# Low halves of weight blocks on GpSimd instead of VectorE, four blocks fewer left unsplit, and one more head searched early

## The chip, the core and the metric

The kernel runs on one core of one Trainium2 chip. The core has five engines that run side by side, each through its own queue in order: TensorE (PE, with its weight loads shown as PEld), VectorE (DVE), ScalarE (ACT), GpSimd (POOL) and SyncE (SP, which only issues DMAs). An engine waits for another by semaphores. The metric is the device time of one execution in microseconds; lower is better.

## The reference

One layer of an encoder block for 512 tokens of width 1024, float32. First a mixer (gated convolution and a gated recurrence in parallel), which ends in a residual add. Then the part that matters here, a retrieval of experts:

```python
q = (xb @ w_q).reshape(p, 8, 2, 64)                      # 8 heads, two half queries
sc = jnp.einsum('phcd,hcnd->phcn', q, sub_keys)           # 128 scores per half
top_s, top_i = lax.top_k(sc, 16)                          # the 16 best of each half
cand_s = top_s[:, :, 0, :, None] + top_s[:, :, 1, None, :]
best_s, best_pos = lax.top_k(cand_s, 16)                  # the 16 best of 256 sums
g = jax.nn.softmax(best_s, axis=-1)
act = gelu(einsum('phkd,pd->phk', expert_u[idx], xb))     # idx: one of 16384 experts
out = einsum('phk,phkd->pd', g * act, expert_v[idx])
```

After it come a residual add and a final normalization.

## The kernel before

*Split products.* The kernel multiplies on PE in a float32 form (FR) that keeps only part of the mantissa. To stay exact it splits a weight block `raw` (128 x 1024) into a high half, the value rounded to FR by an ACT copy (`high`, L75), and a low half, `raw - high`, one subtraction on DVE (`low`, L80). `mm3` then multiplies high by high, high by low and low by high (L89, L90, L91). A block may also stay unsplit: its matmuls in plain float32 (L1039) take longer on PE, but no high or low is needed.

*Phases.* After the mixer, the query phase (L594 to L618): for each of the 8 heads PE projects the queries (`ps_z`), ACT copies them, PE forms the scores (L612), ACT copies those to `sc` (L618; eight buffers, two of them a head). DVE starts on the searches: for one head and one tile of 128 tokens, `top16` finds the 16 best of both halves (MAX8, FIND_INDEX8, MATCH_REPLACE8; L570 to L579; it yields after each of two halves of the work). `early` does this for the first HQ heads and all four tiles. Here a scheduler orders the instructions.

Then the expert phase. The first 64 + 128 tokens (192) are handled sparsely, by gathering expert rows; the other 320 densely: all 128 blocks of `expert_u` are multiplied by the 320 tokens (`u_chunk`), one block of 128 experts each, 123 of them here (block 0 runs in the query phase). Blocks 1 to FN - 1 stay unsplit. Beside them DVE does what is left of the searches (`stage1` for heads HQ to 7, tile 1 first), the selection of each tile (`topk_tile`: candidates L664, best of the candidates, one-hot chains L704 to L709 for the two index halves `ij`, the weights `g`), the gates (one-hot matrices `oh` L755, `igh` L769, multiplied on PE to `ps_gt`, L788, copied by ACT and stored), and the dots of the sparse tokens (L946). POOL gathers expert rows by indirect DMA (`gath`, L925) into five buffers. When `idx_b` (the indices of the first sparse tokens, L715) is planned, the loop emits four gathers. Two loop passes later PE transposes `ij` and `g` (`ps_t`, L730, L731).

Then the vector phase: `expert_v` blocks are weighted into `acc` (L1225), while DVE finishes dots and sums the gathered rows (`ys`, L963).

*What sets the order.* In the expert phase the order is written by a planner in program order: for each block `k` it issues loads, the low of block `k + 2`, the matmuls of `k`, the high of `k + 3`, and then fills DVE from four generators (searches `s`, rest `r`, gates `g`, dots `d`) until DVE's planned time has caught up with PE's. It uses fixed costs:

```python
pe[0] += FPE if c and k < FN else 3530
dve[0] += 0 if c and k < FN - 2 else 1140
while dve[0] < RHO * pe[0] or k == KD:
```

*Buffers.* Raw blocks live in `wraw` (four slots), highs in `whi`, lows in `wlo` (four each). A slot of `wraw` is free for the next load when high and low of its block are formed. Unsplit blocks from number 5 on are loaded into `whi` and `wlo` slots instead.

Of the kernel before, what the change touches and what calls it, by code (L numbers as in the profile page):

```python
# [8 lines left out]
F32 = mybir.dt.float32  # L9
# [25 lines left out]
def block_kernel(ctx, tc, xT, small, w_ada1, w_ada, b_ada, w_in, w_r, w_i, w_out, w_q, keys, uT, u, v, final_g, out):  # L35
    nc = tc.nc
# [31 lines left out]
    def load_w(src):  # L68
        raw = wring.tile([128, KB, 128], F32, name="wraw", bufs=WR)
        nc.sync.dma_start(raw, src)  # L70
        return raw

    def high(raw):
        hi = wring.tile([128, KB, 128], FR, name="whi", bufs=WB)
        nc.scalar.activation(hi, raw, AF.Copy)  # L75
        return hi

    def low(raw, hi):
        lo = wring.tile([128, KB, 128], FR, name="wlo", bufs=WB)
        nc.vector.tensor_sub(lo, raw, hi.bitcast(F32))  # L80
        return lo

    def split_w(raw):
        hi = high(raw)
        return hi, low(raw, hi)

    def mm3(ps, hi, lo, xh, xl, ks, first, last):
        for k in ks:
            nc.tensor.matmul(ps, hi[:, k, :], xh(k), start=first and k == ks[0], stop=False)  # L89
            nc.tensor.matmul(ps, hi[:, k, :], xl(k), start=False, stop=False)  # L90
            nc.tensor.matmul(ps, lo[:, k, :], xh(k), start=False, stop=last and k == ks[-1])  # L91
# [299 lines left out]
    for cb in range(4):  # L391
# [35 lines left out]
        h = mt("ig")  # L427
# [50 lines left out]
    qraw, qsp = {}, {}  # L478
    for m in range(KB):
# [13 lines left out]
        hi, lo = osp.pop(m)  # L493
# [90 lines left out]
    def stage1(heads, tiles):  # L584
        for t in tiles:
            for h in heads:
                yield from top16([(top[:, t, h, c], ti[:, t, h, c], sc[h, c][:, t, :]) for c in range(2)], 128, 1000)

    early = chain(*(stage1([h], range(NT)) for h in range(HQ)))

# [3 lines left out]
    for h in range(8):  # L594
        if h + 2 < 8:
            qraw[h + 2] = load_w(w_q[h + 2])
        else:
            qraw[h + 2] = load_w(uT[h - 6])
        if h:
            qsp[h + 1] = split_w(qraw[h + 1])  # L600
        hi, lo = qsp[h]
        ps = psZ.tile([128, T], F32, name="ps_z", bufs=3)
        mm3(ps, hi, lo, lambda k: h2h[:, k, :], lambda k: h2l[:, k, :], range(KB), True, True)
        if h == 7:
            ps0 = psZ.tile([128, NU], F32, name="ps_z", bufs=3)
            mm3(ps0, *qsp[8], hd, ld, range(KB), True, True)
        qT = qp.tile([128, T], F32, name="qT")
        nc.scalar.activation(qT, ps, AF.Copy)
        pss = [psZ.tile([128, NT, 128], F32, name="ps_g", bufs=2) for c in range(2)]
        for t in range(NT):  # L610
            for c in range(2):
                nc.tensor.matmul(pss[c][:, t, :], qT[64 * c:64 * c + 64, t * 128:(t + 1) * 128],  # L612
                                 keys_sb[64 * c:64 * c + 64, h, :], start=True, stop=True)
        for _ in range(6 if h >= 2 else 0):
            next(early, None)
        for c in range(2):
            sc[h, c] = scs.tile([128, NT, 128], F32, name="sc", bufs=SCB)
            nc.scalar.activation(sc[h, c], pss[c], AF.Copy)  # L618
# [147 lines left out]
    def settle():  # L766
        while lazy:
            o, a, b = lazy.pop(0)
            nc.vector.tensor_tensor(o, a, b, op=OP.mult)  # L769
# [74 lines left out]
    def searches_E():  # L844
        heads = range(HQ, 8)
        yield from stage1(heads, [1])
        yield from topk_tile(1)
        while not gopen:
            yield None
        for t in (2, 3, 0):  # L850
            yield from topk_tile(t)
        sready.append(0)

    def rest_E():
        yield from stage1(range(HQ, 8), [2, 0, 3])
        scx.close()
        stgp.append(ep.enter_context(tc.tile_pool(name="stgp", bufs=1, side="right")))
        gopen.append(cur[0])
# [117 lines left out]
    wraw, whi, wlo = {1: qraw[9]}, {}, {}  # L976
# [3 lines left out]
    def w_load(k):  # L980
        if k < len(jobs):
            kind, i = jobs[k]
            if 5 <= k < FN:
                raw = wring.tile([128, KB, 128], FR, name=("wlo", "whi")[k % 2], bufs=WB).bitcast(F32)
# [11 lines left out]
    def w_high(k):  # L996
        if FN <= k < len(jobs):
            whi[k] = high(wraw[k])

    def w_low(k):  # L1000
        if FN <= k < len(jobs):
            wlo[k] = low(wraw.pop(k), whi[k])
            settle()

    loaded = [4]
# [6 lines left out]
    def weights(k):  # L1012
        w_ahead(k)
        w_low(k + 2)
# [4 lines left out]
    def spill(q):  # L1019
        nc.sync.dma_start(Ad[q], act[q].rearrange("p c t -> p (c t)"))  # L1020
        act[q] = None
# [3 lines left out]
    def u_evict():  # L1025
        if unread:
            c, ps = unread.pop()
            if c % 2 == 0:
                act[c // 2] = ring.tile([128, 2, NU], F32, name="act", bufs=RB // 2)
            nc.scalar.activation(act[c // 2][:, c % 2], ps, AF.Gelu)  # L1030

    def u_chunk(k, pool):
        c = jobs[k][1]
        if c:
            ps = pool.tile([128, NU], F32, name="ps_act", bufs=3 if pool is psE else 2)
            if k < FN:
                raw = wraw.pop(k)
                for j in range(KB):
                    nc.tensor.matmul(ps, raw[:, j, :], h2f[j // 2][:, j % 2], start=j == 0, stop=j == KB - 1)  # L1039
            else:  # L1040
                mm3(ps, whi.pop(k), wlo.pop(k), hd, ld, range(KB), True, True)
            u_evict()
            unread.append((c, ps))
        q = c // 2 - 2
        if c % 2 == 0 and 0 <= q < v0 // 2:
            spill(q)
        pe[0] += FPE if c and k < FN else 3530
        dve[0] += 0 if c and k < FN - 2 else 1140
        ac[0] += 450 if c and k < FN - 3 else 1400

    gbuf, g16, gdone = {}, {}, set()
# [69 lines left out]
    pe, dve, ac = [0], [-HEAD], [0]  # L1121
# [27 lines left out]
    for k in range(1, 3):  # L1149
        w_high(k)  # L1150
    w_low(1)
    manual = ExitStack()
    manual.enter_context(tc.manual_schedule())
    for k in range(CE):
        weights(k)
        u_chunk(k, psE)
        if k >= CE - 2:
            (v_gated, v_high)[k - CE + 2](0)
# [82 lines left out]
    for k in range(CE, len(jobs)):  # L1241
# [5 lines left out]
        if kind == "v" and n % 2:  # L1247
            v_rest(n // 2 + 1)
        w_low(k + 2)
        if kind == "u":  # L1250
            u_chunk(k, psP)
# [71 lines left out]
GS = 32768.0  # L1323
AB = 3
GPE = 460
FN = 12
DX = 0.3
FPE = 4400
SE = 0.65
# [18 lines left out]
WB = 4  # L1348
WR = 4
SCB = 8  # L1350
HQ = 4
VT = 4


# [45 lines left out]
```

## Time and profile before

| | us |
|---|---|
| median of 3 runs | 1334.07 (1334.02 to 1335.56) |
| the profiled execution | 1335.26 |
| its span | 1333.5 |
| PE busy | 1297.6 |
| DVE busy | 1219.9 |
| ACT busy | 728.8 |
| POOL busy | 501.9 |

In the span, the query projections end and the first unsplit block begins at 283.14, and the vector phase begins at 785.9. A line of a time line has start, length, engine, source line, operation, output and inputs, and in brackets the idle time before it with what ended it. A group line has the summed busy time and the mean length in ns. An `x16` behind a matmul counts records: an unsplit block of 8 matmuls has 16.

### The profile page before, as it was taken

The numbers are of one execution on the slowest core, as the hardware profiler recorded it, in microseconds if no ns is written. First come the engines' busy times: TensorE is split into PE (matmuls) and PEld (weight loads), VectorE is DVE, ScalarE is ACT, GpSimd is POOL, SyncE is SP. The second block draws the span as 40 slices with busy tenths as digits, with TensorE's granted clock in tenths as the row PEclk, the third lists the DMA queues.
The fourth block names the chain that finished last, engine by engine and source line by source line (L and its number), as shares of the span: only waits on it lengthen the run. The fifth ranks groups of instructions, "written<-read, shape, count | busy, mean of one in ns | idle before, by whom it ended". The sixth has DMA issues, their size and how long they took to land.

```text
span 1333.5 us, 21104 instructions
## 1 busy us (share of the span) xinstructions
PE 1297.6 (97%) x7408; PEld 1116.0 (84%) x7408; DVE 1219.9 (91%) x2258; ACT 728.8 (55%) x1319; POOL 501.9 (38%) x336
## 2 busy tenths in 40 slices
PE   5999999999899999999999999999999999999996
PEld 2678777777899999999999998888888888888885
DVE  6899876899999999999889769899989989899998
ACT  4667735424686987978659643333343434333333
POOL 0000001000144123456555627677656555555540
PEclk9999999999999999999999999999999999999998
DMA  9684552252799899999999999999999999999993
GB/s 364 228 302 157 165 152 90 69 190 87 254 361 349 316 340 357 390 402 403 418 394 416 418 349 397 390 398 416 412 415 413 415 412 416 412 414 411 412 360 136
DMA packets 150266, 440.03 MB, mean 330 GB/s; under 512 B 16016, under 2 KB 43664, under 8 KB 150160
## 3 DMA queue, kind: packets, MB, share of 16 engines
q1 hardware_dynamic: 103008, 267.23, 53.7%
q0 software_dynamic: 46864, 170.41, 32.4%
q8 instruction: 58, 0.95, 0.3%
q10 hardware_dynamic: 288, 1.05, 0.2%
q14 instruction: 48, 0.39, 0.1%
HBM read 393.54 MB, written 45.09 MB: 329 GB/s over the span
## 4 chain that ended last, share of the span: by engine, by line
PE 74%; DVE 17%; issue 3%; DMA 2%; ACT 2%; POOL 0%; SPq 0%; DVEq 0%; ACTq 0%; POOLq 0%
PE acc L1225 38%; PE ps_act L89 6%; PE ps_act L90 6%; PE ps_act L91 6%; PE ps_z L90 4%; PE ps_z L89 4%; PE ps_z L91 4%; DVE wlo L80 4%; DVE oh L755 2%; DVE scr L946 2%; PE ps_gt L788 2%; DMA wraw<-in_uT_dram 1%; DVE rep L574 1%; DVE igh L769 1%; ACT igh L776 1%
## 5 line engine op out<-in xcount | busy, mean ns | idle before, releaser
L75 ACT ACTIVATE whi<-wraw 128x1024 fp32r<-128x1024 f32 x255 | 269.6, 1058 | 226.7 <-DMA wraw<-in_v_dram 101.4
L80 DVE TENSOR_TENSOR wlo<-wraw,whi 128x1024 fp32r<-128x1024 f32 x255 | 311.1, 1220 | 42.7 <-ACT whi L75 41.7
L89 PE MATMUL ps_act<-h,whi 128*128 128x320 f32 x928 | 292.1, 315 | 0.0
L91 PE MATMUL ps_act<-h,wlo 128*128 128x320 f32 x928 | 287.5, 310 | 0.9 <-DVE wlo L80 0.9
L90 PE MATMUL ps_act<-h,whi 128*128 128x320 f32 x928 | 287.3, 310 | 0.0
L925 POOL DMA_INDIRECT rows<-in_u_dram,idx_s x128 | 206.4, 1612 | 141.7 <-DVE scr L946 112.0
L925 POOL DMA_INDIRECT rows<-in_v_dram,idx_s x128 | 196.6, 1536 | 156.8 <-DVE ys L963 136.1
L1225 PE MATMUL acc<-whi,cl 128*128 128x512 f32 x744 | 229.1, 389 | 0.0
L1225 PE MATMUL acc<-whi,ch 128*128 128x512 f32 x744 | 229.1, 389 | 0.0
L1225 PE MATMUL acc<-wlo,ch 128*128 128x512 f32 x744 | 229.0, 389 | 0.0
L91 PEld LDWEIGHTS ps_act<-h,wlo 128*128 128x128 f32 x928 | 174.6, 188 | 1.3 <-DVE wlo L80 1.1
L89 PEld LDWEIGHTS ps_act<-h,whi 128*128 128x128 f32 x928 | 174.8, 188 | 0.6
L90 PEld LDWEIGHTS ps_act<-h,whi 128*128 128x128 f32 x928 | 174.9, 188 | 0.2
L925 POOL DMA_INDIRECT rows<-in_u_dram,idx_b x64 | 92.5, 1446 | 218.2 <-DVE scr L946 154.9
L963 DVE SCALAR_TENSOR_TENSOR ys<-rows,acts,ys 128x1024 f32<-128x1024 f32 x127 | 163.4, 1287 | 1.4
L1225 PEld LDWEIGHTS acc<-whi,cl 128*128 128x128 f32 x744 | 139.6, 188 | 29.1
L1225 PEld LDWEIGHTS acc<-wlo,ch 128*128 128x128 f32 x744 | 139.6, 188 | 29.0
L1225 PEld LDWEIGHTS acc<-whi,ch 128*128 128x128 f32 x744 | 139.4, 188 | 28.7
L946 DVE SCALAR_TENSOR_TENSOR scr<-rows,h2n 128x1024 f16<-128x1024 f32 x128 | 156.5, 1222 | 4.8 <-DMA rows<-in_u_dram,idx_s 3.2
L1030 ACT ACTIVATE act<-ps_act 128x320 f32<-128x320 f32 x127 | 55.5, 437 | 106.2 <-PE ps_act L91 73.2
L1109 ACT ACTIVATE ch<-cf 128x768 fp32r<-128x768 f32 x64 | 54.2, 847 | 90.9 <-issue 51.8
L776 ACT ACTIVATE igh<-oh,gl 128x128 f16<-128x128 f16 x320 | 99.5, 430 | 7.7 <-DVE oh L755 7.6
(320 smaller groups left out, 1862.6 us busy)
## 6 DMA issues: line engine op xcount, KB each, us to landing
wraw<-in_uT_dram SPq DMA_DIRECT2D x120, 512.0 KB, 7.4
wraw<-in_v_dram SPq DMA_DIRECT2D x103, 512.0 KB, 13.5
Gd<-stg SPq DMA_DIRECT2D x46, 512.0 KB, 9.4
wada<-in_w_ada_dram SPq DMA_DIRECT2D x45, 512.0 KB, 5.3
Ad<-act SPq DMA_DIRECT2D x48, 320.0 KB, 7.7
act<-Ad SPq DMA_DIRECT2D x48, 320.0 KB, 14.4
raw<-in_v_dram SPq DMA_DIRECT2D x25, 512.0 KB, 13.2
h<-Gd SPq DMA_DIRECT2D x12, 1024.0 KB, 17.7
```

The lines of the kernel that those rows point to most:

```text
L75: nc.scalar.activation(hi, raw, AF.Copy)
L80: nc.vector.tensor_sub(lo, raw, hi.bitcast(F32))
L89: nc.tensor.matmul(ps, hi[:, k, :], xh(k), start=first and k == ks[0], stop=False)
L90: nc.tensor.matmul(ps, hi[:, k, :], xl(k), start=False, stop=False)
L91: nc.tensor.matmul(ps, lo[:, k, :], xh(k), start=False, stop=last and k == ks[-1])
L776: nc.scalar.activation(ig[:, 1, k // 2, :, k % 2], of[:, k // 2, 0, :, k % 2], AF.Copy, scale=gl[:, t0 + k:t0 + k + 1])
L925: nc.gpsimd.indirect_dma_start(out=r[:, :], out_offset=None, in_=table, in_offset=bass.IndirectOffsetOnAxis(ap=idxs[:, k:k + 1], axis=0))
L946: nc.vector.scalar_tensor_tensor(scr, rows.pop(n), 1.0, hn, op0=OP.mult, op1=OP.mult, accum_out=dst[:, k:k + 1])
L963: nc.vector.scalar_tensor_tensor(ys, rows.pop(k), acts[:, k:k + 1], ys, op0=OP.mult, op1=OP.add)
L1030: nc.scalar.activation(act[c // 2][:, c % 2], ps, AF.Gelu)
L1109: nc.scalar.activation(ch, coef[q], AF.Copy)
L1225: nc.tensor.matmul(accs[b][e], st[:, bs], mv[:, e * 512:(e + 1) * 512], start=first, stop=last)
```

## The change

The query weights of heads 2 to 7 and block 0 of `expert_u` get their lows on POOL (seven subtractions), and so do blocks 8 to 17 (`k < PL`). FN falls from 12 to 8, so that blocks 8 to 11 are split like the later ones. HQ rises from 4 to 5: the fifth head's four searches move into the query phase, which takes seven search steps a head instead of six. The planner counts no DVE time for the lows on POOL.

```diff
-    def low(raw, hi):
+    def low(raw, hi, eng=None):
         lo = wring.tile([128, KB, 128], FR, name="wlo", bufs=WB)
-        nc.vector.tensor_sub(lo, raw, hi.bitcast(F32))
+        (eng or nc.vector).tensor_sub(lo, raw, hi.bitcast(F32))
...
-            qsp[h + 1] = split_w(qraw[h + 1])
+            qsp[h + 1] = split_w(qraw[h + 1], nc.gpsimd)
...
-        for _ in range(6 if h >= 2 else 0):
+        for _ in range(7 if h >= 2 else 0):
...
-            wlo[k] = low(wraw.pop(k), whi[k])
+            wlo[k] = low(wraw.pop(k), whi[k], nc.gpsimd if k < PL else None)
...
-        dve[0] += 0 if c and k < FN - 2 else 1140
+        dve[0] += 0 if c and k < max(FN, PL) - 2 else 1140
...
-FN = 12
+FN = 8
+PL = 18
...
-HQ = 4
+HQ = 5
```

POOL's queue from the end of the mixer on. `x1d` is the residual stored for the end, `ssum` a zero for one first gather, `idx_b` and `idx_s` the indices of the two sparse groups. Before:

```order
L475 DMA x1d<-xn 128x512 x8
L646 MEMSET ssum 128x8
L647 DMA rows<-in_u_dram,ssum 128x1024
L925 DMA rows<-in_u_dram,idx_b 128x1024 x64
L925 DMA rows<-in_u_dram,idx_s 128x1024 x69
```

Now:

```order
L475 DMA x1d<-xn 128x512 x8
L80 TENSOR_TENSOR wlo<-wraw,whi 128x1024 x7
L646 MEMSET ssum 128x8
L647 DMA rows<-in_u_dram,ssum 128x1024
L80 TENSOR_TENSOR wlo<-wraw,whi 128x1024 x6
L925 DMA rows<-in_u_dram,idx_b 128x1024 x4
L80 TENSOR_TENSOR wlo<-wraw,whi 128x1024 x4
L925 DMA rows<-in_u_dram,idx_b 128x1024 x60
```

The seven lows of the query phase, then those of blocks 8 to 13, stand ahead of the first four gathers; those of blocks 14 to 17 stand between these and the other sixty.

DVE at the end of tile 1's selection, the second one-hot chain (`oh`, `ij`) and the indices. Before:

```order
L579 MAX_INDEX ti<-top,rep 128x8 x2
L80 TENSOR_TENSOR wlo<-wraw,whi 128x1024
L704 TENSOR_TENSOR oh<-oh,io_2644 128x2048
L705 TENSOR_TENSOR oh<-oh,tif 128x2048
L708 TENSOR_TENSOR oh<-oh 128x128x8
L708 TENSOR_TENSOR oh<-oh 128x128x4
L708 TENSOR_TENSOR oh<-oh 128x128x2
L709 TENSOR_TENSOR ij<-oh 128x128
L80 TENSOR_TENSOR wlo<-wraw,whi 128x1024
L712 SCALAR_TENSOR_TENSOR best<-ij 128x128
L715 CAST idx_b<-best 64x64 x2
```

Now:

```order
L574 MATCH_REPLACE rep<-top,sc 128x128 x2
L704 TENSOR_TENSOR oh<-oh,io_2692 128x2048
L705 TENSOR_TENSOR oh<-oh,tif 128x2048
L708 TENSOR_TENSOR oh<-oh 128x128x8
L708 TENSOR_TENSOR oh<-oh 128x128x4
L708 TENSOR_TENSOR oh<-oh 128x128x2
L709 TENSOR_TENSOR ij<-oh 128x128
L712 SCALAR_TENSOR_TENSOR best<-ij 128x128
L715 CAST idx_b<-best 64x64 x2
```

Two lows (of blocks 12 and 13) are gone from this place, and the second half of a search (L577, L579) that stood ahead of the chain now stands behind it.

PE at the transposes of `ij` and `g`; `ps_act_3144` is block 13, `ps_act_3197` block 14. Before:

```order
L91 MATMUL ps_act_3144<-h2_83,wlo_3053 128x320
L730 MATMUL ps_t_3173<-ident_73,ij_2839 128x128 x2
L731 MATMUL ps_t_3173<-ident_73,g_2829 128x128
L89 MATMUL ps_act_3197<-h2_83,whi_3066 128x320
L90 MATMUL ps_act_3197<-h2_83,whi_3066 128x320
L91 MATMUL ps_act_3197<-h2_83,wlo_3089 128x320
```

Now, with `ps_act_3207` block 12 and `ps_act_3244` block 13:

```order
L91 MATMUL ps_act_3207<-h2_83,wlo_3116 128x320
L730 MATMUL ps_t_3236<-ident_73,ij_2862 128x128 x2
L731 MATMUL ps_t_3236<-ident_73,g_2852 128x128
L89 MATMUL ps_act_3244<-h2_83,whi_3145 128x320
L90 MATMUL ps_act_3244<-h2_83,whi_3145 128x320
L91 MATMUL ps_act_3244<-h2_83,wlo_3164 128x320
```

The transposes moved up by one block. The first two gate sets (L788) follow block 17 and block 18 before, and block 16 and block 17 now.

More of the change, by code (lines that the diff above doesn't have):

```diff
@@ L76, in high, with split_w @@
         return hi
-    def low(raw, hi):
+    def low(raw, hi, eng=None):
         lo = wring.tile([128, KB, 128], FR, name="wlo", bufs=WB)
-        nc.vector.tensor_sub(lo, raw, hi.bitcast(F32))
+        (eng or nc.vector).tensor_sub(lo, raw, hi.bitcast(F32))
         return lo
-    def split_w(raw):
+    def split_w(raw, eng=None):
         hi = high(raw)
-        return hi, low(raw, hi)
+        return hi, low(raw, hi, eng)
     def mm3(ps, hi, lo, xh, xl, ks, first, last):
```

## The prediction

> **What bounds the kernel now.** I read first the page's head and busy times, then the work of each stretch, then TensorE's (PE's) waits in the expert phase, then the time lines of PE, VectorE (DVE), ScalarE (ACT) and GpSimd (POOL) where the change sits.
>
> ```profile
> span 1333.5 us, 21104 instructions
> PE 1297.6 (97%) x7408; PEld 1116.0 (84%) x7408; DVE 1219.9 (91%) x2258; ACT 728.8 (55%) x1319; POOL 501.9 (38%) x336
> ```
> ```profile
> 283.14:361.89 78.75, 74.88 (x381) 60.27 (x380) 77.86 (x420) 31.99 (x60) 6.03 (x7) 1.00 0.54 179
> 361.89:470.00 108.11, 107.06 (x843) 105.39 (x841) 107.09 (x227) 88.63 (x186) 36.48 (x25) 1.00 0.92 335
> 470.00:560.00 90.00, 89.53 (x713) 88.09 (x712) 88.68 (x183) 76.30 (x172) 31.29 (x23) 1.00 0.97 360
> 785.90:1310.00 524.10, 524.10 (x2347) 436.01 (x2346) 491.99 (x528) 203.41 (x264) 306.69 (x195) 1.00 1.02 401
> ```
>
> Columns: length, then busy time of PE, PEld, DVE, ACT, POOL, then clock, DMA share, GB/s. From 785.90 on PE never pauses: there nothing but fewer matmuls would help, and the change touches none. In the expert phase before it (from 283.14) PE is nearly full too, and DVE as full; in its first stretch, where the change sits, PE loses 3.87 us. All of PE's visible waits in this phase:
>
> ```profile
> 339.44 0.41 PE L91 MATMUL ps_act<-h,wlo 128*128 128x320 f32 x1 [0.87 <-DVE wlo L80]
> 361.01 1.08 PE L788 MATMUL ps_gt<-igh,oh 128*128 128x128 f16 x16 [3.00 <-DVE igh L769]
> 435.63 1.09 PE L788 MATMUL ps_gt<-igh,oh 128*128 128x128 f16 x16 [0.33 <-ACT stg L798]
> 466.20 1.09 PE L788 MATMUL ps_gt<-igh,oh 128*128 128x128 f16 x16 [0.72 <-DVE igh L769]
> 482.88 1.09 PE L788 MATMUL ps_gt<-igh,oh 128*128 128x128 f16 x16 [0.47 <-DVE igh L769]
> 644.61 1.45 PE L788 MATMUL ps_gt<-igh,oh 128*128 128x128 f16 x10 [1.67 <-ACT igh L776]
> ```
>
> They sum to 7.06 us. So the end moves only by PE's work and by these waits, and I count along PE.
>
> **Four blocks fewer unsplit.** The prices on PE:
>
> ```profile
> 283.14 17.49 PE L1039 MATMUL ps_act<-act,wraw 128*128 128x320 f32 x64
> 300.47 4.47 PE L1039 MATMUL ps_act<-act,whi 128*128 128x320 f32 x16
> 304.77 4.47 PE L1039 MATMUL ps_act<-act,wlo 128*128 128x320 f32 x16
> 337.78 0.38 PE L730 MATMUL ps_t<-ident,ij 128*128 128x128 f32 x2
> 342.77 0.31 PE L89 MATMUL ps_act<-h,whi 128*128 128x320 f32 x1
> 346.29 0.31 PE L89 MATMUL ps_act<-h,whi 128*128 128x320 f32 x1
> 361.89 0.39 PE L89 MATMUL ps_act<-h,whi 128*128 128x320 f32 x1
> ```
>
> and from the page, per group with count, busy time and mean ns, the helpers beside them (evictions L1030, highs L75, dots L946) and the loads' median time to landing:
>
> ```profile
> L75 ACT ACTIVATE whi<-wraw 128x1024 fp32r<-128x1024 f32 x255 | 269.6, 1058 | 226.7 <-DMA wraw<-in_v_dram 101.4
> L946 DVE SCALAR_TENSOR_TENSOR scr<-rows,h2n 128x1024 f16<-128x1024 f32 x128 | 156.5, 1222 | 4.8 <-DMA rows<-in_u_dram,idx_s 3.2
> L1030 ACT ACTIVATE act<-ps_act 128x320 f32<-128x320 f32 x127 | 55.5, 437 | 106.2 <-PE ps_act L91 73.2
> ...
> wraw<-in_uT_dram SPq DMA_DIRECT2D x120, 512.0 KB, 7.4
> ```
>
> An unsplit block takes 304.77 - 300.47 = 4.30 us, a split one (from the first matmul of block 15 to that of block 16) 346.29 - 342.77 = 3.52, a gate set 361.89 - 361.01 = 0.9. Blocks 8 to 11 change: 4 x 0.78 = 3.1 us less PE work. Their four highs go to ACT (busy 31.99 of 78.75 there, so hidden), their lows to POOL. Their loads, formerly into whi/wlo buffers, now take wraw slots after blocks 1 to 4 end, the last at about 300.4; a load lands in 7.4 us and block 11 is due at 283.14 + 7 x 4.30 + 3 x 3.52 = 323.8, so hidden.
>
> **Searches and the selection of tile 1.** This DVE chain ends in `idx_b`, which frees the first gathers, and in `ij` and `g`, which PE transposes.
>
> ```profile
> 239.72 0.48 DVE L570 MAX8 top<-sc 128x8 f32<-128x128 f32 x2
> 283.34 0.17 DVE L639 TENSOR_TENSOR st<-rep 128x16 f16<-128x16 f32 x1 [1.42 <-PE ps_g L612]
> 289.82 0.47 DVE L570 MAX8 top<-sc 128x8 f32<-128x128 f32 x2
> 292.16 0.88 DVE L664 TENSOR_TENSOR oh<-top 128x128 f32<-128x128 f32 x4
> 313.64 1.21 DVE L704 TENSOR_TENSOR oh<-oh,st 128x2048 f16<-128x2048 f16 x1
> 327.57 1.21 DVE L80 TENSOR_TENSOR wlo<-wraw,whi 128x1024 fp32r<-128x1024 f32 x1
> 328.69 1.22 DVE L704 TENSOR_TENSOR oh<-oh,io 128x2048 f16<-128x2048 f16 x1
> 333.18 1.23 DVE L80 TENSOR_TENSOR wlo<-wraw,whi 128x1024 fp32r<-128x1024 f32 x1
> 334.31 0.30 DVE L712 SCALAR_TENSOR_TENSOR best<-ij 128x128 f32<-128x128 f32 x1
> 335.06 0.29 DVE L719 TENSOR_REDUCE ssum<-g 128x8 f32<-128x128 f32 x1
> 335.82 0.48 DVE L570 MAX8 top<-sc 128x8 f32<-128x128 f32 x2
> ```
> ```profile
> 238.43 1.08 ACT L618 ACTIVATE sc<-ps_g 128x512 f32<-128x512 f32 x2
> ```
>
> A search (both halves of one head and tile) is 292.16 - 289.82 = 2.34 us; a low on DVE lasts 328.69 - 327.57 = 1.12 there. Before, 239.72 to 292.16 holds 20 searches (46.8), three lows (3.4), the 1.42 wait and 0.8 of constants. Now DVE can begin when the first half of head 0's scores is out (238.43 + 0.54 = 239.0) and does 23 searches up to the same point, five heads of four tiles and three heads of tile 1: 53.8 + 0.8, with no low and no wait, so 293.6. The selection starts 1.4 us later, although the query lows left DVE: the first ones had stood in time that DVE had free anyway. On PE the query phase costs the same; the buffers that head 7's scores reuse are searched by 239.0 + 16 x 2.34 = 276.4, and those scores come at 283.3. The seven query lows on POOL run beside those projections; without that cover each would stop PE for its own length.
>
> From there to the end of the second one-hot chain (333.18) were 41.0 us; without the low at 327.57, and with 8.5 searches between instead of 9 (order), it is 41.0 - 1.1 - 0.9 = 39.0: `ij` is ready at 332.6, `idx_b` (L712 to L719, 0.7) at 333.3, `g` (L719 to 335.82, 0.8) at 334.1.
>
> **PE meets the transposes one block earlier.** They stood behind block 13, now behind block 12. PE gets there at 283.14 + 7 x 4.30 + 5 x 3.52 = 330.85 and waits for `g` until 334.1: a new wait of 3.2 us, where before (337.78) it found them ready. Block 13 then runs to 337.9.
>
> **Lows 14 to 17 stand behind the gathers.**
>
> ```profile
> 335.30 0.97 POOL L925 DMA_INDIRECT rows<-in_u_dram,idx_b  x1 [49.97 <-DVE idx_b L715]
> 340.49 0.94 POOL L925 DMA_INDIRECT rows<-in_u_dram,idx_b  x1 [0.30 <-issue]
> 0.85 0.23 POOL L53 IOTA ii<- 128x128 int32 x1 [0.40 <-POOLq L1391]
> 1.04 0.23 POOL L58 IOTA iota<- 128x128 f32 x1
> ```
>
> POOL's queue holds four gathers of `idx_b` ahead of the low of block 14. The first waited 0.3 us after `idx_b`, and the fifth began 340.49 - 335.30 = 5.2 us after the first; so low 14 can start only at 333.3 + 0.3 + 5.2 = 338.8, though neither its raw block nor its high waits for that. Block 14 wants it at 337.9 + 0.3 = 338.2. Everything of the four lows, the loads of blocks 18 to 21 (their wraw slots are freed by these lows) and the next 60 gathers queue behind.
>
> What a low costs on POOL no row shows. From below: 1.2 us, the DVE's row. From above: the two iotas follow each other by 0.19 us for 128 columns, 1.5 us for 1024 of one stream; two reads and a write one after another make 4.6. I take 2.4, between one stream and two (1.5 and 3.0) and twice DVE's row. Then low 14 ends at 341.2 and PE waits 3.0 us; lows 15 to 17, each 2.4 against a block's 3.52, are in time. [...]
>
> **Sum.** Up to the second gate set (361.01): -3.1 work, -0.87 and -3.00 of old waits, +3.2 transposes, +3.0 low 14 = -0.8. The old 3.00 goes because DVE gets room: low 18 waits for its load (slot free 341.2, 7.4 to land, high 1.06) and ends near 350.8. Two rounds of one-hot, dot and product with low 19 between (seven instructions, none longer than L946's 1.22) bring the third set's `igh` by 359.3, and PE wants it at 341.2 + 3.3 (the rest of block 14) + 4 x 3.52 + 2 x 0.9 = 360.4: at least 1 us in hand where there was none.
>
> That room should also remove the waits at 466.20 and 482.88 for the same `igh` (0.72 + 0.47 = 1.2). The one on ACT (0.33) and the last (1.67), which follows a late load, I leave. Lows 12 to 17, off DVE too, only make room for dots, whose cost the vector phase hides. Net -0.8 - 1.2 = -2.0 us. The profiled execution took 1335.26 us (1333.5 span and 1.8 around it), 1.2 above the median; I put the difference on the median: 1334.07 - 2.0 = 1332.1.
>
> **Rivals.**
> A, all later waits vanish: -0.8 - 3.2 = -4.0, 1330.1. For it: less DVE work ahead of every gate. Against: the last wait hangs on a load.
> B, DVE and POOL take turns at SBUF. The chain at L704 would start at 293.6 + 21.5 - 0.9 = 314.2; low 11 is ready at about 314.7 (block 7 ends 313.2, its eviction 0.44, a high 1.06). If one low gets in between L704 and L705, DVE loses 2.4 us, `g` and `idx_b` with it, so both new waits move 2.4 later; ACT's second L699, ahead of the highs from block 12 on, follows at about 314.2 + 4.5 (as long as the second chain) + 2.4 = 321.1, still before block 11 needs a bank at 323.8. L755, in front of low 14, adds up to 0.8. Result -2.0 + 3.2 = +1.2, 1335.3. No row has POOL arithmetic beside DVE, so nothing speaks against it. [...]
> C, slower: the low costs near the upper bound. Lows 15 to 17 then outlast the blocks; extra wait (d - 2.4) + 3 (d - 3.52). At 4.6 that is 5.4, so +3.4, 1337.5. It decides from d = 4.4; with B, where DVE loses d too, from 3.2.
> D, gathers crowd the loads. Counted in the order, there are 43 dots ahead of block 58's low instead of 34. Nine gathers of 512 KB at 400 GB/s are 11.8 us of DMA; the stretches 361.89 to 560 leave 0.08 x 108 + 0.03 x 90 = 11.3 free. A wait like 1.67 more: -0.3, 1333.8.
>
> **Numbers.** Forecast 0.33, A 0.17, B 0.27, C 0.13, D 0.10. A change under 0.2% (2.7 us) is about what this measurement can't tell from none. Faster by more: most of A and a fourth of the forecast, 0.25. Slower by more: C, and a part of B and D with a dearer low, 0.23. The rest, 0.52, within. Range 1329 (A and a low at DVE's price) to 1338 (C).
>
> **What would show it.** L730 waiting about 3 us for DVE near 331; L91 waiting about 3 us for POOL's wlo near 338; the selection (L664) starting near 293.6; a POOL low of 2.4 us; no 3 us wait at the second gate set. Wrong if POOL lows last 3.5 us or more, if DVE's two-input instructions stretch or pause beside them, or if the query phase no longer ends near 283.

## The result, and the profile after

The changed kernel takes 1350.13 us (median of 6 runs, 1347.58 to 1353.51), the kernel before 1334.05 beside it (6 runs, 1333.63 to 1335.56): a ratio of 1.0119, with a 95% interval of 1.0104 to 1.0134, 16 us slower. The prediction was 1332.1 us, with a range up to 1338.

The profiled execution took 1350.37 us. First its span and busy times, then the stretch where the change sits (length, then busy time of PE, PEld, DVE, ACT and POOL with the number of instructions, clock, DMA share, GB/s):

```profile
span 1348.4 us, 21172 instructions
PE 1300.0 (96%) x7440; PEld 1121.9 (83%) x7440; DVE 1221.7 (91%) x2245; ACT 729.6 (54%) x1323; POOL 541.5 (40%) x353
282.76:361.89 79.13, 69.20 (x373) 58.97 (x371) 77.96 (x398) 30.04 (x50) 31.50 (x17) 0.98 0.54 163
```

PE lost 10 us in this stretch alone. DVE reads as full as before (77.96 us, 77.86 before), but with 398 instructions instead of 420: it is "busy" over longer instructions, not over more work.

All of PE's waits in the expert phase, from its time line:

```profile
325.22 0.41 PE L89 MATMUL ps_act<-h,whi 128*128 128x320 f32 x1 [1.49 <-ACT act L1030]
336.73 0.33 PE L730 MATMUL ps_t<-ident,ij 128*128 128x128 f32 x1 [4.10 <-DVE ij L709]
338.36 0.48 PE L731 MATMUL ps_t<-ident,g 128*128 128x128 f32 x1 [1.30 <-DVE g L721]
344.85 0.42 PE L91 MATMUL ps_act<-h,wlo 128*128 128x320 f32 x1 [1.11 <-POOL wlo L80]
365.08 1.86 PE L788 MATMUL ps_gt<-igh,oh 128*128 128x128 f16 x16 [5.12 <-DVE igh L769]
373.21 2.31 PE L788 MATMUL ps_gt<-igh,oh 128*128 128x128 f16 x15 [1.89 <-ACT igh L776]
505.69 1.09 PE L788 MATMUL ps_gt<-igh,oh 128*128 128x128 f16 x16 [0.26 <-DVE igh L769]
510.98 1.09 PE L788 MATMUL ps_gt<-igh,oh 128*128 128x128 f16 x16 [0.63 <-DVE igh L769]
613.22 1.09 PE L788 MATMUL ps_gt<-igh,oh 128*128 128x128 f16 x16 [2.87 <-DVE igh L769]
```

They sum to 18.77 us against 7.06, which is 11.7 of the 14.9 us that the span grew. And the loss lies in one place. The evictions of block 12 and block 20 on ACT, one after the other:

```profile
332.56 0.44 ACT L1030 ACTIVATE act<-ps_act 128x320 f32<-128x320 f32 x1 [2.14 <-PE ps_act L91]
384.14 0.44 ACT L1030 ACTIVATE act<-ps_act 128x320 f32<-128x320 f32 x1 [1.16 <-PE ps_act L91]
```

The same two before, from that kernel's time line:

```profile
334.32 0.44 ACT L1030 ACTIVATE act<-ps_act 128x320 f32<-128x320 f32 x1 [2.12 <-PE ps_act L91]
370.20 0.44 ACT L1030 ACTIVATE act<-ps_act 128x320 f32<-128x320 f32 x1 [0.52 <-PE ps_act L91]
```

At block 12 the changed kernel is 1.8 us ahead, eight blocks later 13.9 us behind; behind that point the distance moves between 9 and 21 us, with the gate sets between other blocks, and is 14.0 over the last blocks. What happened in between stands in DVE's and POOL's time lines of the changed kernel:

```profile
301.76 2.47 POOL L80 TENSOR_TENSOR wlo<-wraw,whi 128x1024 fp32r<-128x1024 f32 x1 [16.96 <-ACT whi L75]
302.06 2.25 DVE L682 TENSOR_SCALAR msk<-msk 128x128 uint32<-128x128 uint32 x1
311.48 8.11 POOL L80 TENSOR_TENSOR wlo<-wraw,whi 128x1024 fp32r<-128x1024 f32 x3 [7.26 <-ACT whi L75]
315.79 1.53 DVE L704 TENSOR_TENSOR oh<-oh,st 128x2048 f16<-128x2048 f16 x1
317.36 3.32 DVE L705 TENSOR_TENSOR oh<-oh,dif 128x2048 f16<-128x2048 f16 x1
342.17 10.79 DVE L755 TENSOR_TENSOR oh<-io,selT 128x2048 f16<-128x2048 f16 x1
342.41 9.46 POOL L80 TENSOR_TENSOR wlo<-wraw,whi 128x1024 fp32r<-128x1024 f32 x4
```

Before, L704 and L755 took 1.21 and 1.22 us. Here one L755, a one-hot of the first gates, lasts 10.79 us: it ends 1.1 us behind the last of the four POOL lows beside it, which is about its own length. Summed over the four stretched rows of the expert phase DVE lost 2.0 + 0.3 + 2.1 + 9.6 = 14.0 us (2.25, 1.53, 3.32 and 10.79, less 0.23, which L682 takes without a low beside it in a run below, 1.21, 1.22 and 1.22).

### The profile page after: what moved, and what is told of

Read it like the earlier page. It is cut to its first block, busy times and chain, and to the rows that moved or that the text cites. A ratio compares the mean times of both kernels' runs of the same rounds, so it can differ in the third digit from the quotient of the medians.

```text
span 1348.4 us, 21172 instructions
## 1 busy us (share of the span) xinstructions
PE 1300.0 (96%) x7440; PEld 1121.9 (83%) x7440; DVE 1221.7 (91%) x2245; ACT 729.6 (54%) x1323; POOL 541.5 (40%) x353
## 4 chain that ended last, share of the span: by engine, by line
PE 62%; DVE 23%; DMA 6%; issue 5%; ACT 3%; POOL 0%; DVEq 0%; ACTq 0%; SPq 0%; POOLq 0%
PE acc L1225 32%; PE ps_act L89 5%; PE ps_act L90 5%; PE ps_act L91 5%; DVE wlo L80 4%; PE ps_z L91 4%; PE ps_z L89 4%; PE ps_z L90 3%; DVE scr L946 3%; DVE oh L755 2%; DMA wraw<-in_v_dram 2%; PE ps_gt L788 2%; DVE rep L574 2%; DVE ti L579 1%; DVE ti L572 1%
## 5 line engine op out<-in xcount | busy, mean ns | idle before, releaser
L75 ACT ACTIVATE whi<-wraw 128x1024 fp32r<-128x1024 f32 x259 | 274.0, 1059 | 210.3 <-PE acc L1225 82.3
L80 DVE TENSOR_TENSOR wlo<-wraw,whi 128x1024 fp32r<-128x1024 f32 x242 | 295.3, 1220 | 44.9 <-ACT whi L75 41.9
L89 PE MATMUL ps_act<-h,whi 128*128 128x320 f32 x960 | 303.9, 317 | 1.5 <-ACT act L1030 1.5
L91 PE MATMUL ps_act<-h,wlo 128*128 128x320 f32 x960 | 298.8, 311 | 1.1 <-POOL wlo L80 1.1
L90 PE MATMUL ps_act<-h,whi 128*128 128x320 f32 x960 | 298.8, 311 | 0.0
L925 POOL DMA_INDIRECT rows<-in_v_dram,idx_s x128 | 189.6, 1481 | 170.2 <-DVE ys L963 148.4
L89 PEld LDWEIGHTS ps_act<-h,whi 128*128 128x128 f32 x960 | 182.5, 190 | 2.5 <-ACT act L1030 1.8
L91 PEld LDWEIGHTS ps_act<-h,wlo 128*128 128x128 f32 x960 | 182.0, 190 | 1.4 <-POOL wlo L80 1.4
L90 PEld LDWEIGHTS ps_act<-h,whi 128*128 128x128 f32 x960 | 182.4, 190 | 0.2
L925 POOL DMA_INDIRECT rows<-in_u_dram,idx_b x64 | 96.3, 1505 | 162.4 <-DVE scr L946 146.9
```

The source lines that it names most:

```text
L80: (eng or nc.vector).tensor_sub(lo, raw, hi.bitcast(F32))
L925: nc.gpsimd.indirect_dma_start(out=r[:, :], out_offset=None, in_=table, in_offset=bass.IndirectOffsetOnAxis(ap=idxs[:, k:k + 1], axis=0))
```

## The experiments

The theory after this reading: a POOL low and certain DVE instructions exclude each other, and what DVE loses so is lost to PE in a phase where DVE is full. Rivals: the queue order on POOL (lows behind gathers), the query part, the fifth head, the place of the transposes, the clock. Each run is compared with the kernel before, run on the same chip beside it (medians 1334.16 to 1335.44).

**Lows 14 to 17 back on DVE.**

```diff
-PL = 18
+PL = 14
```

> Lows of blocks 14 to 17 go back to DVE (PL 18 to 14); blocks 8 to 13 and the query weights stay on POOL. Theory (DVE instructions with two SBUF inputs and POOL's subtractions exclude each other, and the four subtractions queued back to back behind the gathers held DVE's L755 for 10.8 us): L755 lasts 1.2 us again, PE's waits of 5.12 and 1.89 us shrink to under 3 together, fewer half-clock windows; the waits near 325 to 338 (1.49, 4.10, 1.30) stay, since blocks 8 to 13 still collide. Time about 1340 (1337 to 1343), 8 to 12 below the changed kernel. Rival (it is the place of the transposes and the later selection, not the exclusion): the transposes still wait some 5 us and the time stays at 1347 to 1350.

Measured: 1338.34 us, ratio 1.0024 [1.0009, 1.0038]. L755 takes 1.22 us again and PE's wait of 5.12 us at the second gate set is gone. Four of the seventeen lows carry 12 of the 16 us. (PL also tells the planner which lows cost DVE time, so DVE's order changes a little too; the run with memsets below keeps it.) What is left: L705 is still 3.32 us (lows 8 to 13 stay on POOL), and PE still waits at the transposes, 4.08 for `ij` and 1.15 for `g`.

**All lows of the expert phase on DVE.**

```diff
-PL = 18
+PL = 0
```

> All lows of the expert phase on DVE (PL 0), with FN 8, five heads early and the query lows on POOL as in the changed kernel. Theory: no DVE instruction of the expert phase is stretched (L682, L705, L755 at 0.2, 1.2, 1.2 us); what is left is 3.1 us less PE work against DVE being later with the selection; 1333 to 1339. Rival (five heads early, or the later start of the selection, cost the time): 1343 or more.

Measured: 1339.56 us, 1.0041 [1.0022, 1.0060], a little above what was expected. No DVE instruction of the expert phase is stretched, L682 for one:

```profile
301.40 0.23 DVE L682 TENSOR_SCALAR msk<-msk 128x128 uint32<-128x128 uint32 x1
314.37 0.41 PE L91 MATMUL ps_act<-h,wlo 128*128 128x320 f32 x1 [1.60 <-DVE wlo L80]
319.97 0.42 PE L91 MATMUL ps_act<-h,wlo 128*128 128x320 f32 x1 [1.82 <-DVE wlo L80]
```

Instead PE waits for the lows of blocks 8 and 9, which are no longer unsplit, and once more for that of block 13 (1.58): on DVE each low costs more (1.2 us) than PE gains by a split block (0.78). Against the next run, which differs only in FN, the four blocks cost 0.2% when split (1.0041 against 1.0022, with intervals that overlap). So "four blocks fewer unsplit" has no good side here: on DVE the lows are late, on POOL they stop DVE.

**The query part alone.** Only the seven query lows on POOL, with five heads searched early:

```diff
-FN = 8
-PL = 18
+FN = 12
+PL = 0
```

> FN 12 and PL 0: only the query lows on POOL and the fifth head early are left of the change. Theory: the query phase ends where it did (283), searches there have one SBUF input and are not stretched, the selection starts 0.5 to 1.5 us later, the expert phase has four searches fewer: 1330 to 1335. Rival (the query part is what costs): 1340 or more, with DVE's two-input instructions or PE's projections stretched before 283.

Measured: 1336.84 us, 1.0022 [1.0007, 1.0037], above the range that was expected. The selection starts at 293.51, where the prediction had 293.6, and low 12 on DVE is 2.67 us late for PE.

**The same with four heads.**

```diff
-HQ = 5
+HQ = 4
...
-        for _ in range(7 if h >= 2 else 0):
+        for _ in range(6 if h >= 2 else 0):
```

> Before, with nothing changed but the seven lows of the query phase on GpSimd: four heads searched early, blocks 1 to 11 unsplit, all later lows on VectorE. Theory (the fifth head's searches ahead of the selection make the selection 1.4 us later, and this is what makes VectorE late at block 13 in the run with five heads, 2.67 us and a half-speed window): the selection (L664) starts at 290.5 to 292.2, no wait above 1.5 us at L91 near 334 to 340, 1332 to 1334.5. Rival (the lows on GpSimd themselves slow VectorE's searches in the query phase): the selection starts at 292.5 or later, 1335 to 1337.

Measured: 1334.09 us, 0.9999 [0.9989, 1.0010]. The selection starts at 292.23, the waits at low 14 (0.87) and at the second gate set (3.02) stay as before. So the seven query lows on POOL cost nothing and bring nothing, as the prediction had it for PE, although one of them meets a DVE instruction too: L268, at the end of the mixer, takes 2.30 us beside the first, where it takes 0.69 otherwise, and the query phase still ends at 283.21. The fifth head costs 0.2% when nothing else is changed (the intervals just overlap).

**Queue order or exclusion.** Lows 14 to 17 replaced by POOL instructions of about the same length at the same place in its queue, which read nothing: two memsets each. The low halves of these four blocks are left out of the computation.

```diff
-            wlo[k] = low(wraw.pop(k), whi[k], nc.gpsimd if k < PL else None)
+            if 14 <= k < PL:
+                wraw.pop(k)
+                wlo[k] = wring.tile([128, KB, 128], FR, name="wlo", bufs=WB)
+                for _ in range(MS):
+                    nc.gpsimd.memset(wlo[k].bitcast(F32), 0.0)
+            else:
+                wlo[k] = low(wraw.pop(k), whi[k], nc.gpsimd if k < PL else None)
...
+MS = 2
```

> The lows of blocks 14 to 17 are not computed: POOL writes each of these tiles with zeros twice (memset), at the same place of its queue, behind the four gathers; the output lacks these blocks' low halves. POOL then writes SBUF but reads nothing. Theory (exclusion through the reading side): L755 beside it lasts 1.2 us, PE's waits of 5.12 and 1.89 shrink as in the run with these lows on DVE, 1338 to 1343. Rival (any POOL work beside DVE stretches it, or it is only POOL's queue): L755 is stretched by about the length of the memsets and the time stays above 1345.

Measured: 1342.86 us, 1.0057 [1.0036, 1.0078]. DVE's L755 and POOL side by side:

```profile
343.61 1.22 DVE L755 TENSOR_TENSOR oh<-io,selT 128x2048 f16<-128x2048 f16 x1
344.03 7.70 POOL L1006 MEMSET wlo<- 128x1024 f32 x8
351.27 0.55 DVE L680 TENSOR_SCALAR msk<-pos 128x128 uint32<-128x128 uint32 x1
```

POOL is busy for 7.70 us at the same place, and L755 is not touched (1.22 us, against 10.79 beside 9.46 us of lows), nor is L769 (0.69 us at 346.43): that POOL works does not by itself stop these two-input instructions. The lows read two tiles and the memsets none, so I take POOL's reading to be what stops them; no run tells it from what else is different between a memset and a subtraction. For DVE instructions of one input not even that much is shown: L680, which takes 0.22 us in the changed kernel, takes 0.55 here and ends with the last memset. The rest of the gap to the run with these lows on DVE (4.5 us) is not taken apart; this run still has the transposes' wait (4.10) and 2.12 us at a gate set.

**Bunched or spread.** The first four gathers no longer stand in a row ahead of low 14, but one ahead of each low.

```diff
-            for m in range(GB_E - 1):
-                gath(u, usteps[m][0], usteps[m][3], m)
+        if first and 0 <= k - first[0] + 4 < GB_E - 1:
+            m = k - first[0] + 4
+            gath(u, usteps[m][0], usteps[m][3], m)
```

> The changed kernel, with the first four gathers no longer in a row ahead of low 14: one gather, low 14, one gather, low 15, and so on to low 17 on GpSimd's queue. Theory (VectorE and GpSimd exclude each other in these instructions, and the waiting VectorE instruction takes its turn as soon as the next GpSimd instruction is no reader of SBUF data): L755 loses one low at most and takes 1.2 to 4.0 us in place of 10.79, the 5.12 wait for igh at L788 and the 1.89 behind it go with their half-speed windows, 1339 to 1343. Rival 1 (VectorE loses the length of all the lows beside it, however they stand): L755 and the next two-input instructions (L769, L755) together still lose about 9 us, 1347 to 1351. Rival 2 (the four gathers, now later, are what counts): VectorE waits for rows at its first dots, 1345 or more with waits named L946.

Measured: 1350.6 us, 1.0125 [1.0108, 1.0142], the same as with the lows bunched. The theory's number (1339 to 1343) fell and rival 1 stood:

```profile
338.57 3.19 DVE L721 TENSOR_TENSOR g<-g,ssum 128x128 f32<-128x128 f32 x1
339.25 2.35 POOL L80 TENSOR_TENSOR wlo<-wraw,whi 128x1024 fp32r<-128x1024 f32 x1
342.73 2.37 POOL L80 TENSOR_TENSOR wlo<-wraw,whi 128x1024 fp32r<-128x1024 f32 x1
343.18 2.68 DVE L664 TENSOR_TENSOR oh<-top 128x128 f32<-128x128 f32 x4
345.79 3.17 DVE L668 CAST tif<-ti 128x256 f16<-128x256 uint32 x1
346.36 2.43 POOL L80 TENSOR_TENSOR wlo<-wraw,whi 128x1024 fp32r<-128x1024 f32 x1
349.91 2.43 POOL L80 TENSOR_TENSOR wlo<-wraw,whi 128x1024 fp32r<-128x1024 f32 x1
350.25 3.19 DVE L755 TENSOR_TENSOR oh<-io,selT 128x2048 f16<-128x2048 f16 x1
```

L755 is down to 3.19 us, but each spread low finds a victim of its own. By the lengths that the same lines have with no low beside them (0.29 and 0.28 for L721 and L668 in the changed kernel, 0.88 and 1.22 before), DVE loses 2.9 + 1.8 + 2.9 + 2.0 = 9.6 us here, to the tenth what the bunched lows took from L755 alone.

**Another victim.** The changed kernel with four heads searched early:

```diff
-HQ = 5
+HQ = 4
...
-        for _ in range(7 if h >= 2 else 0):
+        for _ in range(6 if h >= 2 else 0):
```

> The changed kernel with four heads searched early instead of five (six search steps a head, as before the change); lows on GpSimd and unsplit blocks as changed. Theory (the loss is VectorE blocked by the lows of blocks 8 to 17, about 12 us, and the fifth head adds the 2.8 us that lay between the runs with the query lows alone and five heads, 1.0022, and four heads, 0.9999): 1346 to 1349, with one or more VectorE instructions of over 2 us beside each low. Rival (the fifth head only decides which instruction meets a low): within 1.5 us of 1350.1, or above.

Measured: 1341.02 us, 1.0062 [1.0042, 1.0081], by the ratios some 8 us less than the changed kernel, where the theory had 1 to 4. Five heads or four decides what DVE does when the lows behind the gathers run, which are those of blocks 15 to 17 here (low 14 stands ahead of the gathers):

```profile
342.81 7.12 POOL L80 TENSOR_TENSOR wlo<-wraw,whi 128x1024 fp32r<-128x1024 f32 x3
344.22 0.48 DVE L570 MAX8 top<-sc 128x8 f32<-128x128 f32 x2
344.93 0.29 DVE L572 FIND_INDEX8 ti<-top,sc 128x8 uint32<-128x128 f32 x1
345.45 0.29 DVE L574 MATCH_REPLACE8 rep<-top,sc 128x128 f32<-128x128 f32 x1
346.75 3.93 DVE L664 TENSOR_TENSOR oh<-top 128x128 f32<-128x128 f32 x4
```

It still searches, at full speed in the middle of the lows, and only from 346.75 on does an elementwise instruction (L664) have to wait for their end. These three lows cost DVE 3.0 us here, and L755 (1.22 us at 352.18) meets none; PE still waits 5.10 us at the second gate set. So the loss by a low depends on what it meets: here the search instructions passed (0.48 us for two MAX8, 0.29 for FIND_INDEX8 and for MATCH_REPLACE8), and the elementwise L664 stood still (3.93 us, 0.88 to 0.94 without a low beside it). The rival that I had written down, that the head only decides which instruction meets a low, named the right cause and the wrong size (within 1.5 us of 1350.1).

**The place of the transposes.** Lows 14 to 17 on DVE, and tile 1's transposes a block later:

```diff
-PL = 18
+PL = 14
...
             yield None
             yield None
+            if t == 1:
+                yield None
             pt = psE.tile([128, 4, 128], F32, name="ps_t")
```

> The changed kernel with lows 14 to 17 back on VectorE (1338.34 in the first set) and tile 1's transposes (L730, L731) one block later, where they stood before the change. Theory (the 4.08 + 1.15 us wait there is a matter of place: TensorE reaches them a block of 3.5 us too early, and the long wait brings the half-speed double window behind it): the wait falls to about 1.7 us and at most one half-speed window is left, 1332 to 1335.5. Rival (the gates start a block later and the loss comes back as a wait for igh at L788): waits of 2 to 3 us at the first or third gate set, 1337 to 1340.

Measured: 1336.84 us, 1.0020 [1.0011, 1.0030]. The wait for `ij` falls from 4.08 to 0.60, and PE's waits sum to 6.12 us, less than before the change; still, by the ratios (1.0020 against 1.0024) hardly anything is had back, where 3 to 6 us were expected. From block 18 on this kernel runs between 5 us ahead of the kernel before and 7 us behind, with gates and evictions in another order, and it begins the vector phase at 786.7 (785.8 before).

Two things that the list of waits doesn't show eat up what was won. Where at most one half-speed window was expected, the granted clock is at half for two in a row, 6.83 us from 339.98 on, and PE is busy for 6.00 us of them. And PE is busy longer with the same matmuls of the gate sets. Their group in the kernel before, and here:

```profile
L788 PE MATMUL ps_gt<-igh,oh 128*128 128x128 f16 x768 | 54.3, 220 | 6.3 <-DVE igh L769 4.2 <-ACT igh L776 1.7 <-ACT stg L798 0.3
L790 PE MATMUL ps_gt<-igh,oh 128*128 128x128 f16 x768 | 57.6, 219 | 1.7 <-DVE igh L771 0.8 <-ACT igh L778 0.5
```

Where PE waits for ACT's `igh`, a set is drawn out, in steps too short to be listed as waits: the one at 627.09 has 15 of its matmuls in 2.27 us, where a set mostly takes 1.09. In sum: -3.1 us for the four blocks, -0.9 for the listed waits, +1.3 for the windows (an estimate from the clock of 0.50: half of 6.00, less half of 3.40 before) and +3.3 for the gate sets make +0.6 of the 1.0 us by which the phase is longer here than before.

**The same with four heads.**

```diff
-HQ = 5
+HQ = 4
...
-        for _ in range(7 if h >= 2 else 0):
+        for _ in range(6 if h >= 2 else 0):
```

> The run with lows 14 to 17 on VectorE and the transposes one block later (1336.84), with four heads searched early instead of five. Theory (the fifth head costs about 2.8 us wherever the selection is what TensorE waits for): 1333.5 to 1335.5, the transposes without a wait of over 1 us. Rival (what is left there is the lows of blocks 8 to 13 on VectorE's chain, not the fifth head): 1336 to 1338.

Measured: 1339.56 us, 1.0037 [1.0023, 1.0052]; worse, not better. Low 14, on DVE again, stands behind the whole chain, and PE waits once, but long:

```profile
342.81 0.64 PE L91 MATMUL ps_act<-h,wlo 128*128 128x320 f32 x1 [7.71 <-DVE wlo L80]
```

The fifth head has no price of its own. It moves searches, and the price is that of whatever is late then.

**The half-speed windows.** The granted clock falls to half for 3.4 us after some of the long waits. Two such windows of the changed kernel, and the one of the kernel before (length, busy times, and the mean clock as the third number from the end):

```profile
365.04:368.45 3.41, 3.37 (x22) 3.37 (x22) 3.41 (x5) 3.41 (x6) 0.80 (x1) 0.50 0.55 133
375.28:378.69 3.41, 3.41 (x14) 3.41 (x14) 3.26 (x7) 3.41 (x9) 0.00 (x0) 0.50 0.69 203
```
```profile
645.96:649.38 3.42, 3.40 (x17) 3.14 (x15) 3.42 (x6) 3.42 (x10) 2.21 (x2) 0.50 1.03 419
```

In the one at 375.28 PE's matmuls L89 to L91 start 0.27 us apart, behind it 0.15 us apart. To price the windows, matmuls of the identity fill the wait at the transposes and at the second gate set (their outputs are not used):

```diff
+            for _ in range(WA if t == 1 else 0):
+                nc.tensor.matmul(pt[:, 3, :], ident, ident, start=True, stop=True)
             for w in range(2):
                 nc.tensor.transpose(pt[:, w, :], ij[:, w].rearrange("p h k -> p (h k)"), ident)
...
         pg = psE.tile([128, 4, 128], F32, name="ps_gt", bufs=4)
+        ngt[0] += 1
+        for _ in range(WG if ngt[0] == 3 else 0):
+            nc.tensor.matmul(pg[:, 0, :], ident, ident, start=True, stop=True)
...
+WA, WG = 18, 22
```

> The changed kernel with idle time of TensorE filled: 18 matmuls of the identity by itself (128x128, about 0.19 us each, 3.4 us) ahead of tile 1's transposes, into a quarter of ps_t that nothing else uses, inside the wait of 4.10 us; and 22 (4.2 us) ahead of the third gate set, inside the wait of 5.12, overwritten by the products that follow. All else as in the changed kernel. Theory (a long wait costs its length and also the half-speed window that follows, about 1.7 us for each window that falls on busy time): two or three of the four half-speed windows are gone, the work behind is at full speed, 1344.5 to 1348. Rival (the windows cost next to nothing, since the waits alone set the time): 1349.5 to 1351.5.

Measured: 1351.98 us, 1.0129 [1.0112, 1.0146]: nothing is had back. (What the expectations of these runs call the third gate set is the second.) The rows show why:

```profile
345.47 0.41 PE L91 MATMUL ps_act<-h,wlo 128*128 128x320 f32 x1 [2.33 <-POOL wlo L80]
361.87 5.07 PE L789 MATMUL ps_gt<-ident 128*128 128x128 f32 x44
```

Full speed behind the transposes brings PE to low 14 earlier, and its wait there grows from 1.11 to 2.33; the one for `igh` on ACT grows from 1.89 to 2.28. Here, where the next wait was for POOL or ACT, PE's speed up to it did not count. A price of a window the run does not give: of the four windows of the phase, those at 337.73 and 365.04 are gone, but two others have come, at 346.67 and 735.79. (The 22 matmuls took 5.07 us, not the 4.2 that I had reckoned, so that they held the gates by about a microsecond, which the next wait hid as well.)

**A wait moved.** Could the old 3.00 us at the second gate set of the kernel before be had back by place? The run with the query lows alone and four heads, with one more pass of the loop before the gates go on:

```diff
             if t == 1 and t0 == 64 and scale is None:
                 yield None
+                yield None
```

> Before with the query lows on GpSimd (which measured 0.9999), and the gates of tile 1 from the second set on one block later (one more pass of the loop between them). Theory (a wait of TensorE for igh is a matter of place, and the 3.02 us at the second gate set, with the half-speed window behind it, can be had back by standing later): the 3.0 wait is under 0.5 and no other takes its place, 1330 to 1332.5. Rival (VectorE is full there, 107.09 us of 108.11, so that what is not waited for at the gates is waited for at the next low or set): 1333.3 to 1335.5.

Measured: 1339.10 us, 1.0036 [1.0023, 1.0049], slower than either theory had it. The pass moved DVE's L755 and L769 as well (L769 from 360.36 to 365.60), so the wait came along and grew:

```profile
366.34 1.86 PE L788 MATMUL ps_gt<-igh,oh 128*128 128x128 f16 x16 [4.04 <-DVE igh L769]
```

**Two lows beside searches.** The one arrangement that the theory calls free: query lows on POOL, four heads, blocks 1 to 11 unsplit, and of the expert phase only lows 12 and 13 on POOL, while DVE searches.

```diff
-FN = 8
-PL = 18
+FN = 12
+PL = 14
...
-HQ = 5
+HQ = 4
...
-        for _ in range(7 if h >= 2 else 0):
+        for _ in range(6 if h >= 2 else 0):
```

> Before with the query lows on GpSimd (0.9999) and, of the expert phase, only the lows of blocks 12 and 13 there too; four heads searched early, blocks 1 to 11 unsplit. In the run without these two, their highs are ready at 319.35 and 323.66, VectorE runs MAX8, FIND_INDEX8 and MATCH_REPLACE8 from 318.28 to 327.6, and the two lows stand later on VectorE, 1.12 us each, ahead of the indices and of the first gates. Theory (a GpSimd low stops TENSOR_TENSOR-like instructions and not the search instructions, so that a low beside a search is free): no VectorE instruction is stretched, VectorE's chain is 2.2 us earlier, the 0.87 us wait at low 14 is gone and the 3.02 at the second gate set is about 0.8, 1330.5 to 1332.5. Rival (VectorE is full up to 470 us, and what it gains is waited for elsewhere, as in the run with later gates): 1333.3 to 1336, with new waits at later gate sets.

Measured: 1334.87 us, 1.0007 [0.9997, 1.0016]: no difference from before. The lows are free, as the theory said:

```profile
319.48 2.36 POOL L80 TENSOR_TENSOR wlo<-wraw,whi 128x1024 fp32r<-128x1024 f32 x1 [34.19 <-ACT whi L75]
319.76 0.48 DVE L577 MAX8 top<-rep 128x8 f32<-128x128 f32 x2
323.79 2.36 POOL L80 TENSOR_TENSOR wlo<-wraw,whi 128x1024 fp32r<-128x1024 f32 x1 [1.95 <-ACT whi L75]
327.69 1.21 DVE L704 TENSOR_TENSOR oh<-oh,io 128x2048 f16<-128x2048 f16 x1
344.93 0.46 ACT L1030 ACTIVATE act<-ps_act 128x320 f32<-128x320 f32 x1
```

The second chain starts at 327.69 instead of 328.69, and block 14 is evicted 2.05 us earlier than without these two lows on POOL (346.98). At block 23 (383.38, against 384.11) 0.7 us are left of it, at block 24 nothing, with waits of 0.36 us at low 14 and of 2.61, 0.28, 0.63 and 0.40 at the gates. The time and these waits are as the rival of that run had them: DVE is full up to 470 us, and what it gains it is asked for at the next gate. (Over the last blocks this execution is 1.3 us ahead of the one without the two lows, which the medians do not show.)

## Why the prediction was wrong, step by step

*Right.* A POOL low takes 2.40 us (17 of them, median; 2.4 taken, with some luck, as it was a middle between bounds of 1.2 and 4.6). The query phase ends where it did (282.76). The selection starts at 293.19 (293.6 forecast). At the transposes a wait for DVE appears, 4.10 and 1.30 us (3.2 forecast, 5.6 by rival B), and PE waits for low 14 (1.11; 3.0 forecast). The four blocks gave what they should up to there: 1.8 us ahead at block 12, which is about 3.1 less the 1.49 of the first new wait. That wait the sum did not have. It hangs on DVE as well: ACT's second L699, which stands ahead of the evictions that free PE's `ps_act` buffers, began at 322.93, when DVE's L694 was done; rival B had put it at 321.1, in time for PE.

*The step that failed* is what a POOL low costs DVE. The sum put it at nothing ("Lows 12 to 17, off DVE too, only make room for dots", "The old 3.00 goes because DVE gets room"), though the prediction itself said of rival B that "nothing speaks against it". B, with 0.27, had DVE standing still beside a POOL low, but the wrong size: in the words "one low gets in between L704 and L705, DVE loses 2.4 us" it was right (0.3 and 2.1 us), in "L755, in front of low 14, adds up to 0.8" it was not. L755 lost 9.6 us, B's whole price was 3.2 us on the time, and the four lows 14 to 17 alone carry 12. I had counted one low for L755 and taken for granted that DVE gets its turn after it. In fact it lost to four lows in a row, and where the lows do not stand in a row, four instructions together lose as much. B had L682 (2.0 us) nowhere. The terms that hung on DVE's room then went with it: the old 3.00 us wait at the gates did not go but became 5.12 + 1.89; in place of the waits of 0.72 and 0.47 us, which I had struck out, there are 0.26 and 0.63, and in place of the last, 1.67, there is 2.87.

*One input or two.* The prediction and the expectation of the first run speak of DVE instructions with two inputs, and that of the run with the query part alone gives the searches one. The rows do not divide so. L682 (0.23 us), whose row names one input (`msk`), took 2.25 beside low 8, and the CAST L668 (0.28, from `ti`) took 3.17 in the run with spread lows; MAX8, which has one as well (`sc`), took 0.48 for two among the lows of the changed kernel with four heads, the same as without a low (at 305.01 in the changed kernel). Of FIND_INDEX8 and MATCH_REPLACE8 (0.29 each there, 0.28 and 0.27 without) it is not shown: ahead of each stands a MATCH_VALUE_LOAD of about 0.07 us, and both rows name `top` and `sc`. What sets the search instructions apart, no run here shows.

*A stage that is full has no cover.* The prediction hid POOL's work behind DVE's and DVE's loss behind nothing. From 283 us on DVE is busy 77.86 of 78.75 us, so each microsecond that a POOL low takes from it is late at the next thing that PE asks of it. It held for gains as well: 2.2 us given to DVE (two lows beside searches) were gone ten blocks later.

*Rivals.* A (waits vanish) fell. C (a dear low) fell: 2.40, not 4.6. D (gathers crowd the loads) did not show: no PE wait in the changed kernel is put down to a load.

*Left open.* The phase runs from 282.76 to 799.71 (283.14 to 785.75 before). The sum of the change in waits (+11.7), in PE's other time in it (+2.6) and in what lies around it (+0.6) is the 14.9 us of the span. In that other time, the unsplit blocks give -3.1 and the half-speed windows about +4.8 (an estimate from the clock of 0.50: half of the 2.78, 3.37, 3.41 and 3.41 us that PE is busy in four of them, less half of 3.40 before); the last 0.9 us are not taken apart. The run with the later transposes is 2.7 us slower by the medians; the sum given there covers its phase in one execution, and the rest was not settled. That the exclusion is one of reading rests on one kind of instruction that doesn't read (the memsets, 7.70 us of them beside an L755 of 1.22), and on two-input instructions of DVE only.

No run beat the kernel before.

## What to carry to other kernels

Before moving elementwise work from DVE to POOL, look at what DVE does at those microseconds: beside MAX8 (0.48 us for two), FIND_INDEX8 and MATCH_REPLACE8 (0.29 each) a POOL subtraction was free, beside TENSOR_TENSOR, CAST or TENSOR_SCALAR DVE mostly lost 1.6 to 2.9 us to one subtraction, more than the 1.2 that it had cost on DVE itself. The sign of it was a busy time that stayed the same with fewer instructions (77.96 us with 398, after 77.86 with 420); compare an instruction's length with its neighbours of the same shape. Where an engine was full, as DVE was here (77.86 of 78.75 us), a wait could not be priced alone: taking it away, or moving it, changed which instruction was late next, and only a run told.

## What the hardware showed that I had not expected

A waiting DVE instruction missed its turn between POOL subtractions that stand in a row. L755 stayed out for four of them, 10.79 us, although its row begins 0.24 us before the first. But in the same kernel L704 got in between the second and the third of the three lows from 311.48 on: it ends at 317.32, and the third low takes 3.41 us in place of 2.40, so DVE held up POOL as well:

```profile
316.19 3.41 POOL L80 TENSOR_TENSOR wlo<-wraw,whi 128x1024 fp32r<-128x1024 f32 x1
```

With POOL gathers of 0.95 to 1.09 us between the lows, L721, L664 and L668 each got in after one (3.19, 2.68 and 3.17 us). What decides whose turn it is, no run here shows.

The half-speed clock windows of these runs are 3.4 us long (3.41 and 3.42 above) or two in a row (6.83), and the length of the listed wait did not tell whether one came. In the kernel before, the one at 645.96 follows a wait of only 1.67 us, but behind it the set's 15 matmuls are drawn out over 2.32 us. At the second gate set the clock is full behind a wait of 3.00 us in the kernel before, and at half behind one of 3.02 us in the run with the query lows alone and four heads:

```profile
361.00:364.50 3.50, 3.49 (x34) 3.49 (x34) 3.50 (x12) 3.50 (x10) 0.99 (x1) 1.00 0.51 156
360.51:363.92 3.41, 2.82 (x20) 2.82 (x20) 3.41 (x6) 3.41 (x10) 0.33 (x1) 0.50 0.58 183
```
